# Bidirectional encoder trunk on one core: another order in the last blocks, four joint output operations per head, and a first head that scores a slot later

## The chip, the cores and the metric

The kernel runs on one NeuronCore of a Trainium2 chip. The metric is the device time of one execution in microseconds (us). Engines are named as in the profile: PE is TensorE (PEld its weight loads), DVE is VectorE, ACT is ScalarE, POOL is GpSimd, SP is the engine whose queue issues most DMAs.

## The reference

The input x is 512 tokens by 1024 channels. Two layers are added to it, each as `x = x + layer(x)`, and a last RMSNorm ends it. Layer 0 projects the normed input, runs a gated position mixer and a windowed attention, and projects back. Layer 1, which the change touches, is cut here to what matters:

```python
def hgrn2_direction(q, f_logit, i, lb):        # per head: S, D = 512, 128; chunks
    f = lb + (1.0 - lb) * sigmoid(f_logit); k = 1.0 - f; bcum = cumsum(log(f), within a chunk)
    q_t = q * exp(bcum); k_t = k * exp(-bcum); k_end = k * exp(blast - bcum)
    a = tril(q_t @ k_t.T); o_intra = a @ i
    # state: S = S * exp(blast) + k_end.T @ i;  o_inter = q_t @ S
    return o_intra + o_inter

def odd_layer(x, ...):
    h = rms_norm(x, norm_g); q, f_f, f_b, i, z = split(h @ w_in)      # 16 heads of 128
    o = hgrn2_direction(silu(q), f_f, i) + flip(hgrn2_direction(flip(silu(q)), flip(f_b), flip(i)))
    o = o * rsqrt(mean(o * o, per head) + EPS) * head_norm_g
    return (o * silu(z)) @ w_out

out = rms_norm(x + odd_layer(x, ...), final_norm_g)
```

## The kernel before

Every float32 matrix product is done as three products of parts (hi and lo), on line 207, the "main products". Weights come in pieces of 512 KB: SP issues the load, ACT casts the hi part (L58) and DVE subtracts to get the lo part (L59), some pieces ahead of their use. `t_block` makes 24 main products of 512 columns for one projection of one head, `out_blocks` adds a projection back into x (L254).

Side work is written as generators. Every eighth main product is a slot: `tick` then lets each of up to three side jobs do its next stage, and `yield n` in a job means "n slots from now". So the written order of PE's work is fixed by these numbers; a scheduler then sets the order of each engine's list. Each engine works its list off in order.

In layer 1 (`hgrn`, one job per head) a head needs three `t_block`s, nine slots. Its stages are: a preparation (gate logarithms L608, L611, a scan L614 on DVE, L617, L618, exponentials L622 to L623 on ACT, scalings of keys L628 and L631 on DVE and of queries L630 and L632 on POOL), `yield 7`, scores (L642 to L645) and transposes of keys (L658) with their copies kn (L660), one slot later products L670, one slot later the states u (L678 and L681 on DVE) and products L685, one slot later L689 and L691, then the square (L696), the reduction (L698), the power -0.5 on POOL (L137, L142), the scaling (L700) and the gating (L701), and after four slots the transposes (L705) and the split into hi and lo (L707, L708). For heads 14 and 15 what POOL does is put on DVE (`eng`). Four heads share one pair of value and gate tiles (a group); in each group the main products of the first head come behind those of values and gates.

The end: after head 15 the last two heads are projected by `out_blocks` with `finish` (its squares L151, its sums L155) and `store` (L757, L758), tile of 128 tokens by tile, with DVE's order as written.

Of the kernel before, what the change touches and what calls it, by code (L numbers as in the profile page):

```python
# [10 lines left out]
F32 = mybir.dt.float32  # L11
# [3 lines left out]
AF = mybir.ActivationFunctionType  # L15
ALU = mybir.AluOpType
AX = mybir.AxisListType

P = 128
S = 512  # L20
NT = 4
D = 1024
KT = 8
EPS = 1e-6
# [3 lines left out]
FAR = 1e30  # L28
# [3 lines left out]
class Weights:  # L32
    """Streams weight pieces [128, a, b] with a * b = 1024: DMA, then an exact
    split of every value into two float32r parts (hi + lo)."""
# [50 lines left out]
def tile_encoder(ctx, tc, x, nge, wie, lng, lnb, ws, bs, sink, woe, ngo, wio, gaf, gab, hng, woo, fng, out):  # L85
    nc = tc.nc
    x = x[0]
    out = out[0]
# [8 lines left out]
    def mm_bank():  # L97
        return pm.tile([P, 512], F32, tag="mm", name="mm")
# [4 lines left out]
    W = Weights(tc, wp, dma_ahead=7, split_ahead=3, raw_bufs=4, bufs=4)  # L103

    # ------------------------------------------------ weight order
# [19 lines left out]
    # ------------------------------------------------ constants  # L125
# [14 lines left out]
    def inv_sqrt(v, n, name):  # L140
        r = small.tile([P, n], F32, tag=name + "r", name=name + "r")
        nc.gpsimd.tensor_tensor(out=r, in0=v, in1=mhalf[:, :n], op=ALU.pow)  # L142
        return r
# [5 lines left out]
    def square_half(t, nh, ss, scratch):  # L149
        # (x / 32)^2 summed over 1024 columns: the mean square  # L150
        nc.scalar.activation(scratch, xs[t][:, halves[nh]], AF.Square, scale=1.0 / 32, accum_out=ss[:, nh:nh + 1])  # L151

    def rstd_halves(ss, name):
        v = small.tile([P, 1], F32, tag=name + "v", name=name + "v")
        nc.vector.tensor_scalar(out=v, in0=ss[:, 0:1], scalar1=ss[:, 1:2], scalar2=EPS, op0=ALU.add, op1=ALU.add)  # L155
        return inv_sqrt(v, 1, name)
# [19 lines left out]
    # ------------------------------------------------ blocks of projections  # L176
    # Side work (attention, mixer, recurrence) comes in stages; a stage yields the number of slots of
    # main products to let pass before the next one, so that the tensor engine doesn't wait for it.
# [25 lines left out]
    def mm3(ps, ops):  # L204
        n = len(ops)
        for i, (l, r) in enumerate(ops):
            nc.tensor.matmul(ps, lhsT=l, rhs=r, start=(i == 0), stop=(i == n - 1))  # L207
            count[0] += 1
            if count[0] % SLOT == 0:
                tick()  # L210
# [50 lines left out]
    def split_act(src):  # L261
        """float32 [128, 512] in SBUF -> hi + lo"""
        ahi, alo = act_pair()
        nc.scalar.copy(ahi, src)
        nc.vector.tensor_tensor(out=alo, in0=src, in1=ahi.bitcast(F32), op=ALU.subtract)
        return ahi, alo

    # ================================================ layer 0
# [30 lines left out]
    with ExitStack() as c0:  # L299
# [37 lines left out]
        # the order in which the loads arrive  # L337
# [23 lines left out]
        # distance |s - t| of key column c (s = c - 128) to query row t, out of the window: FAR  # L361
# [13 lines left out]
        # ---- position mixer weights, transposed to [s, g, t]  # L375
# [8 lines left out]
        # ---- v_a and its LayerNorm  # L384
# [22 lines left out]
        # ---- keys and values  # L407
# [18 lines left out]
        # ---- attention  # L426
# [80 lines left out]
        # ---- spatial gating  # L507
# [28 lines left out]
    # ================================================ layer 1  # L536
    l1 = ctx.enter_context(tc.tile_pool(name="l1", bufs=1, reuse_waits="tile"))

    # ---- lower bounds: rows (direction, layer, head) then the head norm's gains, transposed to [d, row]
# [25 lines left out]
    # ---- masks  # L565
# [3 lines left out]
    # scores of a chunk, s on partitions: rows of its first half A hold A -> A, A -> B forwards and the  # L569
    # extra A -> A backwards; rows of its second half B hold B -> A, B -> B backwards and the extra B -> B forwards  # L570
# [12 lines left out]
    # ---- end of layer 0: its last products, with the norm of each tile of tokens as it is complete  # L583
# [5 lines left out]
    sst = {}  # L589
# [12 lines left out]
    def hgrn(h, sq, sg, iv, zv):  # L602
# [30 lines left out]
        yield 7  # L633
# [18 lines left out]
        # ---- states, centred in the middle of each chunk; step j: chunk j forwards, chunk 3 - j backwards  # L652
# [47 lines left out]
        nc.vector.tensor_tensor(out=o2, in0=pov, in1=r.unsqueeze(2).broadcast_to([P, NT, P]), op=ALU.mult)  # L700
        eng.tensor_tensor(out=o2, in0=o2, in1=zv[:, :, hs], op=ALU.mult)  # L701
# [40 lines left out]
    def finish(t, nh):  # L742
        if nh == 0:
            sst[t] = small.tile([P, 2], F32, tag="ss", name="ss")
        junk = l1.tile([P, 512], F32, tag="o2", name="junk", bufs=1)
        square_half(t, nh, sst[t], junk)
        if nh == 1:
            if t:
                store(t - 1)
            scales.append(rstd_halves(sst[t], "nr"))  # L750

    scales = []

    def store(t):
        for cs in halves:
            xv = xs[t][:, cs]
            nc.vector.scalar_tensor_tensor(out=xv, in0=xv, scalar=scales[t], in1=gain2[:, cs], op0=ALU.mult, op1=ALU.mult)  # L757
            nc.sync.dma_start(out=out[ts(t, P), cs], in_=xv)  # L758
# [4 lines left out]
    with tc.manual_schedule(engines={mybir.EngineType.DVE}):  # L763
        out_blocks([acat1[14], acat1[15]], finish)
        store(NT - 1)
# [29 lines left out]
```

## Time and profile before

| | |
|---|---|
| device time, median of 3 runs (lowest to highest) | 1036.95 us (1036.91 to 1037.04) |
| span of the profiled execution | 1035.3 us |
| mean granted clock of PE over the span | 0.997 |
| DMA, fastest of the 40 slices of the span | 322 GB/s |
| stores of the output | 8 of 256 KB, 2.1 us from issue to landing |

The profiled execution's own device time is not among the three runs; what lies around its span is taken from the median, 1.65 us. The page shows the busy share of each engine, and its longer part groups of instructions by line. The views used below are the list of waits (who waited for whom), and the timeline, in which every row is an instruction with its start, its duration, its engine and line, what it writes and reads, and in brackets how long its engine had been idle before it and what ended that.

### The profile page before, as it was taken

The page shows a single profiled execution, that of the slowest core. Times are in us where ns is not written, and L with a number is a line of the kernel's source. Part 1 is how long each engine was busy: PE and PEld are TensorE (multiplying, and loading weights), DVE is VectorE, ACT ScalarE, POOL GpSimd, SP SyncE. Part 2 cuts the span into 40 slices and gives each one's busy share as a digit, 9 for nine tenths or more (in the row PEclk, how much of TensorE's full clock was granted, in tenths as well). Part 3 has the DMA queues.
Part 4 walks back from the last instruction along what each step waited for, and adds up shares of the span by engine and source line. Part 5 has one row for each costly group of instructions (what it writes and reads, how often), then busy time and mean ns, then how long its engine had stood idle before and what let it go on. Part 6 is the DMA issues. An engine that isn't in the chain of part 4 may idle for free.

```text
span 1035.3 us, 13564 instructions
## 1 busy us (share of the span) xinstructions
PE 1012.9 (98%) x5381; PEld 851.9 (82%) x5381; DVE 597.7 (58%) x946; ACT 517.1 (50%) x705; POOL 147.4 (14%) x155
## 2 busy tenths in 40 slices
PE   6999999999999999999999999999999999999996
PEld 5888888888888887888888888888888888878884
DVE  6574677566434464446754546754436764547685
ACT  5333666354222144458743258753257753377742
POOL 1140000000000200004231003322002322012101
PEclk9999999999999999999999999999999999999998
DMA  9243222222233222341212432212432223422102
GB/s 322 85 120 85 81 62 62 82 82 82 82 85 99 85 81 82 100 131 54 85 39 82 122 102 62 63 61 82 122 102 61 62 62 102 122 82 77 47 1 81
DMA packets 109343, 90.05 MB, mean 87 GB/s; under 512 B 2992, under 2 KB 88544, under 8 KB 109280
## 3 DMA queue, kind: packets, MB, share of 16 engines
q1 hardware_dynamic: 109184, 89.14, 28.3%
q8 instruction: 42, 0.69, 0.3%
q14 instruction: 21, 0.17, 0.1%
q0 software_dynamic: 96, 0.04, 0.0%
HBM read 87.08 MB, written 2.10 MB: 86 GB/s over the span
## 4 chain that ended last, share of the span: by engine, by line
PE 89%; ACT 3%; DVE 3%; issue 2%; POOL 1%; DMA 1%; SPq 0%; POOLq 0%; DVEq 0%; ACTq 0%
PE mm L207 74%; PE sm L670 2%; PE sm L642 2%; PE sm L448 1%; PE sm L685 1%; PE sm L487 1%; PE sm L691 1%; PE sm L689 1%; DVE c L614 1%; PE sm L476 1%; PE sm L658 1%; PE sm L705 1%; PE sm L512 1%; PE sm L644 1%; ACT whi L58 1%
## 5 line engine op out<-in xcount | busy, mean ns | idle before, releaser
L59 DVE TENSOR_TENSOR wlo<-wraw,whi 128x1024 fp32r<-128x1024 f32 x156 | 196.9, 1268 | 143.9 <-ACT whi L58 141.5
L58 ACT CAST whi<-wraw 128x1024 fp32r<-128x1024 f32 x156 | 163.1, 1051 | 231.2 <-PE mm L207 215.0
L207 PE MATMUL mm<-hlo,whi 128*128 128x512 f32 x656 | 258.2, 394 | 0.0
L207 PE MATMUL mm<-hhi,wlo 128*128 128x512 f32 x656 | 257.8, 393 | 0.0
L207 PE MATMUL mm<-hhi,whi 128*128 128x512 f32 x656 | 256.5, 391 | 0.0
L207 PEld LDWEIGHTS mm<-hhi,whi 128*128 128x128 f32 x656 | 123.3, 188 | 24.6
L207 PEld LDWEIGHTS mm<-hlo,whi 128*128 128x128 f32 x656 | 123.3, 188 | 24.1
L207 PEld LDWEIGHTS mm<-hhi,wlo 128*128 128x128 f32 x656 | 123.3, 188 | 23.9
L207 PE MATMUL mm<-whi,hhi 128*128 128x512 f32 (+1 forms) x352 | 135.9, 386 | 0.1
L207 PE MATMUL mm<-whi,hlo 128*128 128x512 f32 (+1 forms) x352 | 135.5, 385 | 0.0
L207 PE MATMUL mm<-wlo,hhi 128*128 128x512 f32 (+1 forms) x352 | 135.3, 385 | 0.0
L207 PE MATMUL mm<-whi,ahi 128*128 128x512 f32 x256 | 100.4, 392 | 0.1
L207 PE MATMUL mm<-wlo,ahi 128*128 128x512 f32 x256 | 100.3, 392 | 0.0
L207 PE MATMUL mm<-whi,alo 128*128 128x512 f32 x256 | 100.1, 392 | 0.0
L207 PEld LDWEIGHTS mm<-wlo,hhi 128*128 128x128 f32 x352 | 66.6, 189 | 13.1 <-DVE wlo L59 1.1
L207 PEld LDWEIGHTS mm<-whi,hhi 128*128 128x128 f32 x352 | 66.8, 190 | 12.6 <-ACT hhi L170 0.7
L207 PEld LDWEIGHTS mm<-whi,hlo 128*128 128x128 f32 x352 | 66.5, 189 | 12.0 <-DVE hlo L171 0.3
L254 DVE TENSOR_TENSOR x<-mm,x 128x512 f32<-128x512 f32 x72 | 49.0, 688 | 43.5 <-PE mm L207 43.4
L630 POOL TENSOR_TENSOR sq<-sq,en 128x512 f32<-128x512 f32 x14 | 23.8, 1700 | 266.4 <-ACT en L622 266.4
L207 PEld LDWEIGHTS mm<-whi,ahi 128*128 128x128 f32 x256 | 48.1, 188 | 10.2 <-ACT ahi L707 0.5
L207 PEld LDWEIGHTS mm<-whi,alo 128*128 128x128 f32 x256 | 48.1, 188 | 9.6
L207 PEld LDWEIGHTS mm<-wlo,ahi 128*128 128x128 f32 x256 | 48.1, 188 | 9.5
(176 smaller groups left out, 1377.2 us busy)
## 6 DMA issues: line engine op xcount, KB each, us to landing
wraw<-in_w_in_odd_dram SPq DMA_DIRECT2D x80, 512.0 KB, 3.9
wraw<-in_w_in_even_dram SPq DMA_DIRECT2D x44, 512.0 KB, 4.0
wraw<-in_w_out_even_dram SPq DMA_DIRECT2D x16, 512.0 KB, 3.5
wraw<-in_w_out_odd_dram SPq DMA_DIRECT2D x16, 512.0 KB, 3.5
x<-in_x_dram SPq DMA_DIRECT2D x4, 512.0 KB, 8.3
out_dram<-x SPq DMA_DIRECT2D x8, 256.0 KB, 2.1
pThi<-in_norm_g_even_dram SPq DMA_DIRECT2D x1, 512.0 KB, 5.4
lngb<-in_gmlp_ln_g_dram SPq DMA_DIRECT2D x1, 512.0 KB, 6.1
```

The costliest lines, as they stand in the source:

```text
L58: self.nc.scalar.copy(hi, raw)
L59: self.nc.vector.tensor_tensor(out=lo, in0=raw, in1=hi.bitcast(F32), op=ALU.subtract)
L207: nc.tensor.matmul(ps, lhsT=l, rhs=r, start=(i == 0), stop=(i == n - 1))
L254: nc.vector.tensor_tensor(out=xv, in0=ps, in1=xv, op=ALU.add)
L448: nc.tensor.matmul(pv, lhsT=a[:, ql], rhs=b[:, kv, kr], start=(i == 0), stop=(i == 2))
L476: nc.tensor.transpose(ps[:, ts(n - n0, P)], pr[:, n, ts(j - KEYS[n][0], P)], ident)
L487: nc.tensor.matmul(po[:, n0 * P:n1 * P], lhsT=a[:, j, ts(kv, P)], rhs=b[:, j, :w], start=(j == 0 and i == 0), stop=(j == NT - 1 and i == 2 ...
L512: nc.tensor.matmul(ps[:, ts(n, P)], lhsT=va[n][:, ts(c, P)], rhs=wsT[:, g], start=True, stop=True)
L614: nc.vector.tensor_tensor_scan(out=cf, data0=reset.rearrange("p n t -> p (n t)"), data1=cf, initial=0.0, op0=ALU.mult, op1=ALU.add)
L630: eng.tensor_tensor(out=v8(qb), in0=v8(qf), in1=en[:, 1, :, 0:64], op=ALU.mult)
L642: nc.tensor.matmul(ps[:H, o:o + P], lhsT=kf[:, lo_:mid], rhs=qf[:, lo_:hi_], start=True, stop=True)
L670: nc.tensor.matmul(ps[:, ts(2 * j + d, P)], lhsT=kn[:, jj, d], rhs=iv[:, n, hs], start=True, stop=True)
```

## The change

Three edits. A first head of a group (`hl == 0`) lets eight slots pass before its scores, not seven. A head's output is scaled and gated in four joint DVE operations of 128 columns, one per tile of tokens, in place of L700 and L701. And `finish` and `store` are replaced by `last_blocks`, in which the scaling of a finished tile is shared among DVE, ACT and POOL, the last block of PE is cut in two of 256 columns, and the last store goes out in two halves, one on ACT's DMA queue; ACT's order is now as written there, too. Comments that went are left out here.

```diff
-        yield 7
+        yield 8 if hl == 0 else 7
...
-        nc.vector.tensor_tensor(out=o2, in0=pov, in1=r.unsqueeze(2).broadcast_to([P, NT, P]), op=ALU.mult)
-        eng.tensor_tensor(out=o2, in0=o2, in1=zv[:, :, hs], op=ALU.mult)
+        for n in range(NT):
+            nc.vector.scalar_tensor_tensor(out=o2[:, n], in0=pov[:, n], scalar=r[:, n:n + 1], in1=zv[:, n, hs],
+                                           op0=ALU.mult, op1=ALU.mult)
...
+        def part(t, i, c0, n):
...
+            mm3(ps[:, :n], ops)
+            xv = xs[t][:, c0:c0 + n]
+            nc.vector.tensor_tensor(out=xv, in0=ps[:, :n], in1=xv, op=ALU.add)
+            nc.scalar.activation(junk[:, :n], xv, AF.Square, scale=1.0 / 32, accum_out=sums[t][:, i:i + 1])
+
+        def scale_of(t):
+            v = small.tile([P, 1], F32, tag="nrv", name="nrv")
+            ss = sums[t]
+            nc.vector.tensor_scalar(out=v, in0=ss[:, 0:1], scalar1=ss[:, 1:2], scalar2=EPS, op0=ALU.add, op1=ALU.add)
+            if t == NT - 1:
+                nc.vector.tensor_scalar(out=v, in0=ss[:, 2:3], scalar1=v, scalar2=None, op0=ALU.add)
+            scales[t] = inv_sqrt(v, 1, "nr")
+
+        def store(t):
+            x0, x1 = xs[t][:, :512], xs[t][:, 512:]
+            nc.vector.scalar_tensor_tensor(out=x0, in0=x0, scalar=scales[t], in1=gain2[:, :512], op0=ALU.mult, op1=ALU.mult)
+            nc.sync.dma_start(out=out[ts(t, P), :512], in_=x0)
+            nc.scalar.activation(x1, x1, AF.Copy, scale=scales[t])
+            nc.gpsimd.tensor_tensor(out=x1, in0=x1, in1=gain2[:, 512:], op=ALU.mult)
+            nc.sync.dma_start(out=out[ts(t, P), 512:], in_=x1)
+
+        for t in range(NT):
+            sums[t] = small.tile([P, 4], F32, tag="ss", name="ss")
+            part(t, 0, 0, 512)
+            if t:
+                scale_of(t - 1)
+            if t < NT - 1:
+                part(t, 1, 512, 512)
+            else:
+                part(t, 1, 512, 256)
             if t:
                 store(t - 1)
...
+        t = NT - 1
+        part(t, 2, 768, 256)
+        xg = [l1.tile([P, 512], F32, tag=tag, name="xg", bufs=1) for tag in ("u", "kn1")]
+        nc.vector.tensor_tensor(out=xg[0], in0=xs[t][:, :512], in1=gain2[:, :512], op=ALU.mult)
+        scale_of(t)
+        nc.vector.tensor_tensor(out=xg[1], in0=xs[t][:, 512:], in1=gain2[:, 512:], op=ALU.mult)
+        nc.scalar.activation(xg[0], xg[0], AF.Copy, scale=scales[t])
+        nc.vector.tensor_scalar(out=xg[1], in0=xg[1], scalar1=scales[t], scalar2=None, op0=ALU.mult)
+        nc.sync.dma_start(out=out[ts(t, P), 512:], in_=xg[1])
+        nc.scalar.dma_start(out=out[ts(t, P), :512], in_=xg[0])
```

In the changed kernel the lines from L701 on have other numbers: the joint operation is L701, the transposes of the output L706, the split L708 and L709, the gate's sigmoid L739, and of the end the add L761, the square L762, the sums L767 and L769, the scalings L774 (DVE), L776 (ACT) and L777 (POOL), and of the last tile L794, L796, L797 and L798.

The list of DVE before, from the first head's weight split to the second head's scan (u: states of the first head; sg and c: gates of the second; wlo: a weight piece):

```order
L59 TENSOR_TENSOR wlo<-wraw,whi 128x1024
L681 TENSOR_SCALAR u<-sm,tt 128x128 x2
L678 TENSOR_TENSOR u<-sm,u 128x256
L681 TENSOR_SCALAR u<-u,tt 128x128 x2
L678 TENSOR_TENSOR u<-sm,u 128x256
L681 TENSOR_SCALAR u<-u,tt 128x128 x2
L611 TENSOR_SCALAR sg<-sg,noml,oml 128x512
L614 SCALAR_TENSOR_TENSOR c<-reset,c 128x1040
L617 COPY tt<-c 128x16
L618 TENSOR_TENSOR c<-c,tt 128x8x65
```

The same place in DVE's list of the changed kernel:

```order
L59 TENSOR_TENSOR wlo<-wraw,whi 128x1024
L681 TENSOR_SCALAR u<-sm,tt 128x128 x2
L678 TENSOR_TENSOR u<-sm,u 128x256
L611 TENSOR_SCALAR sg<-sg,noml,oml 128x512
L614 SCALAR_TENSOR_TENSOR c<-reset,c 128x1040
L681 TENSOR_SCALAR u<-u,tt 128x128
L617 COPY tt<-c 128x16
L681 TENSOR_SCALAR u<-u,tt 128x128
L618 TENSOR_TENSOR c<-c,tt 128x8x65
L678 TENSOR_TENSOR u<-sm,u 128x256
L681 TENSOR_SCALAR u<-u,tt 128x128 x2
```

The second head's gate operations and its scan stood behind the last state and now stand between the first and the second. The four groups have the same list there.

ACT's list of the changed kernel at the same place, from the second head's first logarithm L608 (kn: transposed keys of the first head; whi: a weight piece; o: square of the first head's output):

```order
L608 ACTIVATE c<-sg,lb,oml 128x8x64
L739 ACT_TABLE_LOAD
L739 ACTIVATE sg<-mm 128x512
L660 COPY kn_3765<-sm 128x512
L660 COPY kn_3765<-sm 128x256
L58 CAST whi<-wraw 128x1024
L608 ACT_TABLE_LOAD
L608 ACTIVATE c<-sg,lb,oml 128x8x64
L622 ACT_TABLE_LOAD
L622 ACTIVATE en<-c 128x1040
L625 ACTIVATE tt<-tt 128x16
L623 ACTIVATE c<-c 128x1040
```

Before, the two copies kn and the cast stood ahead of the sigmoid and its table load, and the square L696 stood ahead of L622; now L696 comes behind L623, the sigmoid of the third head's query and one more cast.

POOL's list of the changed kernel at the end (nrr: power of a tile's mean square; x: a tile of the output):

```order
L142 TENSOR_TENSOR nrr<-nrv,mhalf 128x1
L777 TENSOR_TENSOR x_70<-x_70,gain_7759 128x512
L142 TENSOR_TENSOR nrr<-nrv,mhalf 128x1
L777 TENSOR_TENSOR x_71<-x_71,gain_7759 128x512
L142 TENSOR_TENSOR nrr<-nrv,mhalf 128x1
L777 TENSOR_TENSOR x_72<-x_72,gain_7759 128x512
L142 TENSOR_TENSOR nrr<-nrv,mhalf 128x1
```

Before, POOL had the four powers L142 there and nothing between them.

## Rows read from the trace of the kernel before

**Rows 1.** The page, part 1: busy us (share of the span) x instructions.

```profile
PE 1012.9 (98%) x5381; PEld 851.9 (82%) x5381; DVE 597.7 (58%) x946; ACT 517.1 (50%) x705; POOL 147.4 (14%) x155
```

**Rows 2.** List of waits, PE: line, released by; us in total, times, longest us.

```profile
PE sm L642 <- POOL sq L632: 4.1, 4, 1.0
```

**Rows 3.** Timeline of PE, first group: start, us, engine, line, out<-in, [idle before <-releaser].

```profile
470.62 0.32 PE L642 MATMUL sm<-sq,sg 128*64 128x128 f32 x1 [1.03 <-POOL sq L632]
...
474.68 1.50 PE L670 MATMUL sm<-iv,kn 128*128 128x128 f32 x12
...
480.60 0.38 PE L689 MATMUL sm<-u,sq 128*128 128x128 f32 x2
...
481.86 0.48 PE L207 MATMUL mm<-hlo,whi 128*128 128x512 f32 x1
...
491.02 0.60 PE L705 MATMUL sm<-ident,o 128*128 128x128 f32 x4
```

**Rows 4.** Timeline of ACT, first group.

```profile
472.48 0.82 ACT L608 ACTIVATE c<-sg,lb,oml 128x512 f32<-128x512 f32 x1
473.20 0.84 ACT L660 COPY kn<-sm 128x512 f32<-128x512 f32 x2
474.64 1.04 ACT L58 CAST whi<-wraw 128x1024 fp32r<-128x1024 f32 x1 [0.60 <-PE mm L207]
475.70 1.28 ACT L738 ACT_TABLE_LOAD   x1
477.00 0.60 ACT L738 ACTIVATE sg<-mm 128x512 f32<-128x512 f32 x1
...
485.98 1.08 ACT L623 ACTIVATE c<-c 128x1040 f32<-128x1040 f32 x1
```

**Rows 5.** Timeline of DVE, first group.

```profile
475.72 1.23 DVE L59 TENSOR_TENSOR wlo<-wraw,whi 128x1024 fp32r<-128x1024 f32 x1 [1.78 <-ACT whi L58]
476.86 0.73 DVE L681 TENSOR_SCALAR u<-sm,tt 128x128 f32<-128x128 f32 x2
477.62 0.42 DVE L678 TENSOR_TENSOR u<-sm,u 128x256 f32<-128x256 f32 x1
...
479.25 0.60 DVE L681 TENSOR_SCALAR u<-u,tt 128x128 f32<-128x128 f32 x2
...
480.22 2.32 DVE L614 TENSOR_TENSOR_SCAN c<-reset,c 128x1040 f32<-128x1040 bf16 x1
...
482.78 0.70 DVE L618 TENSOR_TENSOR c<-c,tt 128x520 f32<-128x520 f32 x1
483.40 0.68 DVE L698 TENSOR_REDUCE hss<-o 128x4 f32<-128x512 f32 x1
```

**Rows 6.** Timeline: POOL in the first group, and beside DVE behind it.

```profile
484.43 1.03 POOL L142 TENSOR_TENSOR hrr<-hrv,mhalf 128x4 f32<-128x4 f32 x1 [9.11 <-DVE hrv L137]
...
489.29 1.30 POOL L701 TENSOR_TENSOR o<-o,zv 128x512 f32<-128x512 f32 x1
...
554.80 1.21 DVE L59 TENSOR_TENSOR wlo<-wraw,whi 128x1024 fp32r<-128x1024 f32 x1
555.03 2.13 POOL L701 TENSOR_TENSOR o<-o,zv 128x512 f32<-128x512 f32 x1 [0.87 <-DVE o L700]
```

**Rows 7.** Timeline of the end, all engines.

```profile
1014.60 0.69 DVE L700 TENSOR_TENSOR o<-sm,hrr 128x512 f32<-128x512 f32 x1 [1.19 <-POOL hrr L142]
...
1016.64 0.63 PE L705 MATMUL sm<-ident,o 128*128 128x128 f32 x4 [0.91 <-DVE o L701]
...
1020.29 0.63 ACT L151 ACTIVATE junk<-x 128x512 f32<-128x512 f32 x1 [2.30 <-DVE x L254]
...
1022.09 0.56 POOL L142 TENSOR_TENSOR nrr<-nrv,mhalf 128x1 f32<-128x1 f32 x1 [7.52 <-DVE nrv L155]
...
1026.11 0.39 PE L207 MATMUL mm<-whi,alo 128*128 128x512 f32 x1
...
1030.60 1.42 DVE L757 SCALAR_TENSOR_TENSOR x<-x,nrr,gain 128x512 f32<-128x512 f32 x2 [0.66 <-POOL nrr L142]
```

More of the change, by code (lines that the diff above doesn't have):

```diff
@@ L741, in tile_encoder, with last_blocks @@
     nc.sync.dma_start(out=gain2, in_=fng.partition_broadcast(P))
-    def finish(t, nh):
-        if nh == 0:
-            sst[t] = small.tile([P, 2], F32, tag="ss", name="ss")
+    def last_blocks(heads):
+        pieces = [W.take() for _ in range(2)]
         junk = l1.tile([P, 512], F32, tag="o2", name="junk", bufs=1)
-        square_half(t, nh, sst[t], junk)
-        if nh == 1:
+        sums, scales = {}, {}
+        def part(t, i, c0, n):
+            ps = mm_bank()
+            ops = []
+            nh, cs = c0 // 512, slice(c0 % 512, c0 % 512 + n)
+            for k, (ahi, alo) in enumerate(heads):
+                whi, wlo = pieces[nh]
+                a, b = ahi[:, ts(t, P)], alo[:, ts(t, P)]
+                ops += [(a, whi[:, k, cs]), (a, wlo[:, k, cs]), (b, whi[:, k, cs])]
+            mm3(ps[:, :n], ops)
[25 more added lines that the diff above has]
+                part(t, 1, 512, 256)
@@ L748, in finish @@
             if t:
                 store(t - 1)
[L750 to L758, printed above, removed]
+        t = NT - 1
+        part(t, 2, 768, 256)
+        xg = [l1.tile([P, 512], F32, tag=tag, name="xg", bufs=1) for tag in ("u", "kn1")]
@@ L762, in tile_encoder @@
     tick_until(lambda: 15 in acat1)
-    with tc.manual_schedule(engines={mybir.EngineType.DVE}):
-        out_blocks([acat1[14], acat1[15]], finish)
-        store(NT - 1)
+    with tc.manual_schedule(engines={mybir.EngineType.DVE, mybir.EngineType.Activation}):
+        last_blocks([acat1[14], acat1[15]])
 _INS = ['x', 'norm_g_even', 'w_in_even', 'gmlp_ln_g', 'gmlp_ln_b', 'gmlp_w_s', 'gmlp_b_s', 'attn_sink',
```

## The prediction

> **What bounds the kernel now.** I read the engine shares of the page first: the TensorE (PE) is busy for 1012.9 of 1035.3 us, every other engine for 58% or less [rows 1]. So a microsecond counts only where PE waits, or after PE's last product. The list of waits, for PE, has one entry in layer 1 that repeats: the score products L642 wait for POOL's second scaling of the queries (L632), 4.1 us in four waits, 1.0 each at most [rows 2]. They are the first heads of the four groups; the other twelve heads score without a wait. The PE timeline around the first of them shows a gap of 1.03 us before L642 at 470.62 [rows 3]. Last I read the end: PE waits once more, 0.91 us, for the last head's output (L705 at 1016.64), starts its last product at 1026.11, and VectorE (DVE) ends its last scaling at 1030.60 + 1.42 = 1032.02 [rows 7]; the rest to 1035.3 is the last store and the program's end. So the change aims at three places where time really is lost: 4.1 us at the first heads, about 1 us at the last head, and 6 us behind the last product.
>
> **First heads, one slot later.** Eight main products go ahead of the scores. Forty of them take 491.02 - 481.86 = 9.16 us [rows 3], so eight take 1.83 us, more than the 1.03 us of the gap: the wait for POOL goes. The price stands in the instruction order. The first head's later steps (states, L670; u, L681 and L678; L689 and L691) also come one slot later, but the second head's preparation does not. Before, DVE did the whole u chain of the first head (476.86 to 479.25 + 0.60 = 479.85) and then the second head's L611 and scan L614 [rows 5]. Now L611, L614, L617 and L618 stand inside the u chain. DVE and ACT work through their lists in order, so I replay them from the trace, on the clock of the first group.
>
> PE: without a new wait L689 would start at 480.60 - 1.03 + 1.83 = 481.40 [rows 3], L691 and the other products around it take 481.86 - 480.60 = 1.26, and the main products would go on at 482.66.
>
> ACT: nothing is changed up to L608, which ends at 472.48 + 0.82 = 473.30. Then before came the copies kn (L660) [rows 4]; now a table load (1.28) and the gate's sigmoid (0.60, as L738 had) come first, so kn is complete at 473.30 + 1.28 + 0.60 + 0.84 = 476.02. The next weight cast L58 (1.04) ends at 477.06. PE wants kn's first part for L670 at 474.68 - 1.03 + 1.83 = 475.48 and gets it some 0.3 later, a small wait that the next one swallows.
>
> DVE: the weight split L59 stands ahead of u and waits for that cast, as it did before (475.72, released by ACT); u starts 476.86 - 475.72 = 1.14 later, at 478.20. L678 follows after 477.62 - 476.86 = 0.76, at 478.96; L611, behind it, needs the second sigmoid's L608, which ends at 477.06 + 1.28 + 0.82 = 479.16, so that it starts at about 479.4, and takes some 0.45 to the scan. From the scan's start to L618 it is 482.78 - 480.22 = 2.56 [rows 5], with two u scalings of 0.30 between; then L618 about 0.62, L678 about 0.46 and the last pair L681 0.60: 479.85 + 2.56 + 0.60 + 0.62 + 0.46 + 0.60 = 484.69. L691 can follow at about 484.8 and the main products at 485.0, where 482.66 was wanted: a wait of 2.3 us in place of the 1.03. Against before, where eight products more would have brought PE to 481.86 + 1.83 = 483.69, each group is 1.3 us later. If DVE overlaps its small operations better than I add them, u ends 0.3 earlier, and it is 1.0.
>
> A second chain holds PE to the same. ACT's exponentials wait for L618 (now at about 483.7): table load 1.28, L622 and L623 some 1.1 each [rows 4], load 1.28, sigmoid 0.60, cast 1.04, and only then the square L696 (0.60): 490.7. DVE's L59 before the reduction ends at about 491.3, the reduction takes about 0.7 [rows 5], L137 0.2, POOL's power 1.0 [rows 6], and the joint operations come at 493.3 to 494.7. PE is at the transposes at 485.0 + 9.16 = 494.2, its fourth at 494.5: a wait of 0 to 0.4. So a quicker u alone would not win the time back. I take 1.25 a group, from 1.0 to 1.7; the order is the same in all four, so 4 x 1.25 = +5.0 us (+4.0 to +6.8).
>
> **Output of a head in four joint operations.** L700 (0.69) and the gating (1.30 on POOL, 0.68 on DVE for heads 14 and 15) become four operations of 128 columns on DVE. None of that form stands in the trace; from the 512-wide L700 (0.69) a quarter each gives at least 0.17, a 128-wide scaling that reads PSUM (two L681 in 0.73) at most 0.41 [rows 5 and 7]. I take 0.35, as this is the nearest form: 1.4 us for four. For heads 0 to 13 it costs nothing: DVE is busy 58%, PE does not wait for these outputs before, and POOL loses 1.3 us of work. For head 15 it counts: before, 1014.60 to 1016.64; now the fourth output is there at about 1016.0 and the fourth transpose starts at 1016.2, where it started at about 1016.97: 0.75 us earlier (0.5 to 1.3).
>
> **The last blocks.** They are in another order, too: eight instead of twelve products of head 14 stand ahead of the first product with head 15. The four missing ones (0.23 each, 0.9 us) come behind it, so that PE's last product ends at about 1026.5, as before (1026.11 + 0.39), and the 0.75 us are gone. Behind it DVE has less to do: half of each store's scaling is ACT's and POOL's. But POOL's list now alternates L142 and L777, so each tile's power waits for the multiplication of the tile before. PE ends tile 1's second block 24 products of 0.23 before its end, at 1021.0; its add (0.7, as L700) and its square with the sum read out (0.8) bring 1022.5. From there: ACT's scaling of tile 0 0.60, L777 1.30 (POOL's L701 has that shape, [rows 6]), L142 0.56 [rows 7], to 1025.0; tile 1 likewise (its power is used after tile 2's squares, 1025.2), 1025.2 + 0.6 + 1.3 + 0.56 = 1027.7; then DVE scales tile 2 (0.7), and only behind that adds the last quarter, which PE had ready since 1026.5: 1028.8. Then L794 reads two SBUF operands beside L777 of tile 2 (1028.4 to 1029.7). In the trace such a pair was not run together: POOL's L701 took 2.13 instead of 1.30 when it met L59 [rows 6], about the rest of L59 longer. So L794 ends at 1030.4; L767 and L769 0.3, L142 0.6 with its start, the last scalings 0.6: 1032.0, where before had 1032.02. I take 0 for the end. Best case, with no collision and short operations, -1.5; worst, with each L777 at 2.13 (two on the chain, 1.7, less the 0.9 of slack at L794) and the two last stores sharing the DMA engines (0.8, a store's 256 KB at the 322 GB/s of the page's fastest slice), some +1.5.
>
> The Trainium skill, page "SBUF — State Buffer", section "Who interferes with whom", says that a VectorE instruction with two SBUF inputs and a GpSimd instruction that reads SBUF exclude each other for the whole instruction. The pair in [rows 6] agrees: 555.03 + 2.13 is 1.15 us after L59's end at 556.01. By the rule L794 waits as reckoned, and without it the end would be 0.9 us earlier.
>
> **Sum.** The profiled execution has a span of 1035.3; the runs' median is 1036.95, so 1.65 us lie around it. 1035.3 + 5.0 + 0 + 1.65 = 1041.95 us.
>
> **Rivals.** (1) The wait just goes: 4 x 1.03 = -4.1 us, 1032.8, faster. For it: the gap of the list of waits is real, and u, ready at 479.85 for a last use at about 481.7, had 1.8 us of room. Against: scan, L617 and L618 add 3.2 us. It decides if u, with all that is put into it, ends before 482.4, 2.3 us earlier than I reckon: 0.07. (2) u comes late by just what was won, 1.25 us a group less than I reckon: 1036.95, no change; it needs L59 ahead of u not to wait for the late cast, which the row at 475.72 speaks against: 0.07. (3) More comes with it: after the late transposes the second head's scores follow at once, where a slot lay between, and its last transposes wait until DVE has emptied the PSUM bank of the first ones; at 1.9 us a group and +1 at the end it gives 1036.95 + 8.6 = 1045.5: 0.08. (4) The end runs at PE's pace, because POOL's products are shorter than reckoned: -1.5, with the groups' +5.0: 1040.5; it lies within my forecast.
>
> **How the numbers follow.** The forecast (with 4) has 0.78. Its own range is 1035.3 + 1.65 + 4.0 - 1.5 = 1039.4 to 1036.95 + 6.8 + 1.5 = 1045.3 if all ends meet; I cut it to 1039.0 to 1044.2, which leaves out rivals 1 and 2 and most of 3, about 0.2. About 0.2% (2.1 us) is what a measurement of this kernel can tell from no change. Faster by that: 0.08. Within: 0.08, mostly rival 2. Slower: 0.84.
>
> **What would show it.** In the profile after: PE's wait at L642 for POOL gone from the list, and four new waits of about 2 us at L689 or L691, released by DVE's u (L681), with scan L614 between the u rows; L660 behind a sigmoid; a wait of some tenths at L706. At the end: L777 of about 1.3 us on POOL ahead of each L142, and the last scaling ending about 1032 plus the shift. No PE wait at L691, and a span of about 1031, would make my replay of DVE's list wrong; a span of 1033 with the waits there would mean an end that is 7 us shorter than I think.

## The result

The changed kernel took 1042.45 us (median of four runs, 1041.74 to 1042.72) against 1036.93 of the kernel before in the same session: a ratio of 1.0052, 95% interval 1.0038 to 1.0067. It is slower, by 5.5 us, where 5.0 were forecast. Its profiled execution took 1042.44 us with a span of 1040.4; all starts below are of profiled executions, counted from the start of the span. The traces of the experiments e1 and e9 are not used, since every main product in them took several times its usual duration; their timed runs are.

The engine shares [rows 1] have hardly moved; PE has most of its time, as before:

```profile
PE 1017.1 (98%) x5387; PEld 853.6 (82%) x5387; DVE 598.1 (57%) x992; ACT 519.5 (50%) x711; POOL 132.0 (13%) x144
```

The list of waits does show the change (line, what it waited for, us in all, times, longest). The entry for POOL's scaling L632 of [rows 2] is gone; u has come in its place:

```profile
PE sm L689 <- DVE u L681: 3.3, 4, 0.8
PE sm L706 <- DVE o L701: 1.0, 1, 1.0
PE sm L670 <- ACT kn L660: 0.8, 4, 0.2
```

The timeline of PE in the first group answers to [rows 3] (start, us, line, out<-in, and in brackets the idle time and what ended it):

```profile
475.69 1.60 PE L670 MATMUL sm<-iv,kn 128*128 128x128 f32 x12 [0.19 <-ACT kn L660]
...
481.74 0.38 PE L689 MATMUL sm<-u,sq 128*128 128x128 f32 x2
...
483.86 0.49 PE L689 MATMUL sm<-u,sq 128*128 128x128 f32 x2 [0.84 <-DVE u L681]
484.18 0.42 PE L691 MATMUL sm<-u,sq 128*128 128x128 f32 x2
...
493.33 0.39 PE L207 MATMUL mm<-hhi,whi 128*128 128x512 f32 x1
493.56 0.67 PE L706 MATMUL sm<-ident,o 128*128 128x128 f32 x4
...
496.34 0.47 PE L207 MATMUL mm<-hlo,whi 128*128 128x512 f32 x1
```

The list gives 0.84 us to the wait for u, but the starts tell more: from the first of the products with u to the last it is 484.18 - 481.74 = 2.44 us, where the trace of before has 1.11 (from the 480.60 of [rows 3] to 481.71). So 1.33 us are lost here, some more at L670, and the 1.03 of [rows 2] is won. At the transposes (L706, 493.56) the list names no wait; the second head's scores now follow them at once, and from the last main product ahead of both to the first behind them it is 496.34 - 493.33 = 3.01 us. ACT and DVE in the same stretch, against [rows 4] and [rows 5]:

```profile
474.57 0.60 ACT L739 ACTIVATE sg<-mm 128x512 f32<-128x512 f32 x1
475.06 0.86 ACT L660 COPY kn<-sm 128x512 f32<-128x512 f32 x2
...
478.03 0.72 DVE L681 TENSOR_SCALAR u<-sm,tt 128x128 f32<-128x128 f32 x2
...
479.58 2.32 DVE L614 TENSOR_TENSOR_SCAN c<-reset,c 128x1040 f32<-128x1040 bf16 x1
...
483.46 0.60 DVE L681 TENSOR_SCALAR u<-u,tt 128x128 f32<-128x128 f32 x2
...
492.71 1.13 DVE L701 SCALAR_TENSOR_TENSOR o<-sm,hrr,zv 128x128 f32<-128x128 f32 x4 [1.14 <-POOL hrr L142]
```

The sigmoid stands ahead of kn, and the second head's scan (479.58, 2.32 us) stands inside the first head's u chain, which ends at 483.46 + 0.60 = 484.06 instead of 479.85. The square of the output (L696) of the second to fourth head comes 0.78 us later than before in the first group, 1.90 in the second, 2.95 in the third, 4.02 to 4.08 in the last: the groups cost 4.08 us, and not all of that is the slot's (e3).

The end, against [rows 7]. The square of the last head starts at 1015.98 (before: 1011.90), so from there to the span's end it is 24.4 us after and 23.4 before, 1.0 more:

```profile
1029.94 1.27 POOL L777 TENSOR_TENSOR x<-x,gain 128x512 f32<-128x512 f32 x1 [0.91 <-ACT x L776]
...
1030.21 0.28 PE L207 MATMUL mm<-whi,alo 128*128 128x256 f32 x1
...
1031.18 0.55 POOL L142 TENSOR_TENSOR nrr<-nrv,mhalf 128x1 f32<-128x1 f32 x1
...
1031.76 0.75 DVE L774 SCALAR_TENSOR_TENSOR x<-x,nrr,gain 128x512 f32<-128x512 f32 x1 [0.89 <-POOL nrr L142]
...
1032.56 1.26 POOL L777 TENSOR_TENSOR x<-x,gain 128x512 f32<-128x512 f32 x1 [0.83 <-ACT x L776]
...
1032.76 1.61 DVE L794 TENSOR_TENSOR xg<-x,gain 128x512 f32<-128x512 f32 x1
...
1034.90 0.93 POOL L142 TENSOR_TENSOR nrr<-nrv,mhalf 128x1 f32<-128x1 f32 x1 [1.07 <-DVE nrv L769]
...
1035.86 0.49 DVE L798 TENSOR_SCALAR xg<-xg,nrr 128x512 f32<-128x512 f32 x1 [0.44 <-POOL nrr L142]
...
1036.61 0.37 ACTq L800 DMA_DIRECT2D out_dram<-xg  x1
```

PE's last product has moved by 1030.21 - 1026.11 = 4.10, just with the groups. Behind it the last tile's first product with the gains (L794) takes 1.61 us beside POOL's L777, the last power (L142) 0.93 beside L796, where those of the tiles before took 0.55 to 0.57.

### The profile page after: what moved, and what is told of

The parts are those of the page before. It is cut to its first block, busy times and chain, and to the rows that moved or that the text cites. A ratio compares the mean times of both kernels' runs of the same rounds, so it can differ in the third digit from the quotient of the medians.

```text
span 1040.4 us, 13601 instructions
## 1 busy us (share of the span) xinstructions
PE 1017.1 (98%) x5387; PEld 853.6 (82%) x5387; DVE 598.1 (57%) x992; ACT 519.5 (50%) x711; POOL 132.0 (13%) x144
## 4 chain that ended last, share of the span: by engine, by line
PE 84%; ACT 7%; DVE 5%; issue 2%; POOL 1%; DMA 1%; POOLq 0%; SPq 0%; ACTq 0%; DVEq 0%
PE mm L207 71%; DVE c L614 2%; PE sm L670 2%; ACT L739 1%; PE sm L448 1%; PE sm L487 1%; ACT whi L58 1%; PE sm L642 1%; PE sm L685 1%; DVE wlo L59 1%; PE sm L689 1%; PE sm L691 1%; PE sm L476 1%; PE sm L706 1%; ACT sg L739 1%
## 5 line engine op out<-in xcount | busy, mean ns | idle before, releaser
L59 DVE TENSOR_TENSOR wlo<-wraw,whi 128x1024 fp32r<-128x1024 f32 x156 | 192.0, 1235 | 143.0 <-ACT whi L58 140.6
L207 PEld LDWEIGHTS mm<-hhi,wlo 128*128 128x128 f32 x656 | 123.3, 188 | 24.4
L207 PE MATMUL mm<-whi,ahi 128*128 128x512 f32 (+1 forms) x258 | 100.8, 391 | 0.0
L207 PE MATMUL mm<-wlo,ahi 128*128 128x512 f32 (+1 forms) x258 | 100.8, 391 | 0.0
L207 PE MATMUL mm<-whi,alo 128*128 128x512 f32 (+1 forms) x258 | 100.3, 390 | 0.0
L254 DVE TENSOR_TENSOR x<-mm,x 128x512 f32<-128x512 f32 x64 | 43.9, 688 | 42.7 <-PE mm L207 42.6
```

Source lines behind the costliest of these rows:

```text
L59: self.nc.vector.tensor_tensor(out=lo, in0=raw, in1=hi.bitcast(F32), op=ALU.subtract)
L254: nc.vector.tensor_tensor(out=xv, in0=ps, in1=xv, op=ALU.add)
```

## The experiments

Each was timed in five rounds beside the kernel before (1036.67 us in the session of e1 to e4, 1036.89 in that of e5 to e8, 1036.88 in that of e9 to e11).

| run | us | ratio to before, 95% interval |
|---|---|---|
| e1 changed, without the slot | 1038.98 | 1.0020, 1.0011 to 1.0029 |
| e2 slot alone | 1050.99 | 1.0138, 1.0125 to 1.0152 |
| e3 joint operations alone | 1036.54 | 0.9999, 0.9990 to 1.0007 |
| e4 changed, second head a slot later too | 1039.97 | 1.0030, 1.0018 to 1.0043 |
| e5 e4, scan held behind u | 1041.61 | 1.0049, 1.0036 to 1.0062 |
| e6 e3, first heads' queries on DVE | 1033.12 | 0.9967, 0.9955 to 0.9979 |
| e7 e1, no multiplications on POOL at the end | 1037.94 | 1.0011, 1.0002 to 1.0020 |
| e8 e1, last store on SP's queue | 1038.94 | 1.0021, 1.0012 to 1.0030 |
| e9 slot and joint operations | 1039.64 | 1.0028, 1.0017 to 1.0040 |
| e10 new last blocks alone | 1038.47 | 1.0018, 1.0009 to 1.0027 |
| e11 first heads' queries on DVE alone | 1033.67 | 0.9971, 0.9960 to 0.9982 |

**e1, the slot taken back**

```diff
-        yield 8 if hl == 0 else 7
+        yield 7
```

> The changed kernel with the slot taken back: the first heads are scored after 7 slots again, the joint output operations and the new last blocks stay. Theory (the slot costs 4.08 us over the four groups, the last blocks 1.0, the joint operations nothing): the four waits of 1.03 us at the score products for POOL's scaling are back, no wait at u's products, and the time is 1036.93 + 1.0 = 1037.9 us. Rival A (the last blocks cost nothing by themselves and were only pushed by the late groups): 1036.9. Rival B (the slot costs nothing and what lies around it is late through the output operations): 1042.4.

Measured: 1038.98 us. The slot costs 1042.45 - 1038.98 = 3.5 us of the 5.5, and the rest costs 2.3, not the 1.0 that the theory gave it. So neither rival is right. The 1.0 was the end's difference against before, and the joint operations had paid a part of it (e3).

**e2, the slot alone**

```diff
-        yield 7
+        yield 8 if hl == 0 else 7
```

> The kernel before with the slot alone: first heads scored after 8 slots, the output in its old form (a scaling on DVE, the gating on POOL), the old last blocks. Theory: u's wait comes as in the changed kernel (+4.08 in all), and the old output form, which in the changed kernel's trace would end at about 492.71 + 0.69 + 1.30 + 0.1 = 494.8 where PE wants it at 493.3 to 493.6, adds a wait of about 1.3 us at the transposes of each group's first head: 1036.93 + 4.1 + 5.2 = 1046.2 us, with four such waits for POOL in the list. Rival A (no coupling of slot and output form): 1041.0 and no wait at these transposes. Rival B (the slot alone is a gain of its wait): 1032.8.

Measured: 1050.99 us, 14 us slower, more than any theory had. The coupling is there, and larger than reckoned. From the list of waits, and the timeline of POOL and DVE ahead of the first transposes:

```profile
PE sm L705 <- POOL o L701: 7.9, 4, 2.0
```

```profile
493.15 1.22 DVE L59 TENSOR_TENSOR wlo<-wraw,whi 128x1024 fp32r<-128x1024 f32 x1
...
493.38 2.11 POOL L701 TENSOR_TENSOR o<-o,zv 128x512 f32<-128x512 f32 x1 [0.87 <-DVE o L700]
...
494.29 1.49 DVE L611 TENSOR_SCALAR sg<-sg,noml,oml 128x512 f32<-128x512 f32 x1
```

PE waits 2.0 us for each first head's output, not 1.3: the gating on POOL (L701) meets the weight split L59 on DVE and takes 2.11 instead of the 1.30 of [rows 6], and DVE's L611 behind it takes 1.49, where it took 0.54 elsewhere. From the last main product ahead of the first transposes to the first behind the scores, it is 5.05 to 5.10 us in the second to fourth group and 6.63 in the first, where the changed kernel takes 3.0: 9.8 us more in all. The 1.5 that the first group has more are the clock's, in this row of the view of windows (stretch, its length, busy us and instructions of PE, PEld, DVE, ACT and POOL, granted clock, DMA share, GB/s):

```profile
497.00:499.00 2.00, 2.00 (x27) 1.88 (x25) 1.37 (x3) 0.00 (x0) 0.00 (x0) 0.50 0.23 84
```

Behind the wait, in which PE did nothing for 2.0 us, the granted clock fell from 1.00 to 0.50 (the lower of its two levels, 1.2 of 2.4 GHz), and the scores ran at that pace. In the other three groups it stayed at 1.00 behind the same wait; why it fell in the first alone is open. So in the changed kernel the joint operations hide most of the slot's harm.

**e3, the joint operations alone**

```diff
-        nc.vector.tensor_tensor(out=o2, in0=pov, in1=r.unsqueeze(2).broadcast_to([P, NT, P]), op=ALU.mult)
-        eng.tensor_tensor(out=o2, in0=o2, in1=zv[:, :, hs], op=ALU.mult)
+        for n in range(NT):
+            nc.vector.scalar_tensor_tensor(out=o2[:, n], in0=pov[:, n], scalar=r[:, n:n + 1], in1=zv[:, n, hs], ...)
```

> The kernel before with the joint output operations alone. Theory: no PE wait changes for heads 0 to 14; the last head's transposes come 0.75 us earlier, and the end of the kernel before follows PE, so that the time is 1036.93 - 0.7 = 1036.2 us, and the wait at the last transposes falls from 0.91 to some 0.2 us. Rival (more work on DVE delays other steps, four small operations cost more than one large): 1037.5 or more, with new waits for DVE.

Measured: 1036.54 us, no difference that can be told. Its trace has two effects that work against each other. From the first head's square to the last's it takes 0.7 us more (0.2 at each of the three changes of group), and from the last head's square to the end it takes 1034.4 - 1012.08 = 22.3 us instead of 23.4: the last scalings start at 1029.73 instead of 1030.60 [rows 7]. At a change of group a weight load of PE (PEld) waits for a weight split; then PE's last product and these scalings:

```profile
555.96 0.19 PEld L207 LDWEIGHTS mm<-wlo,hhi 128*128 128x128 f32 x1 [0.34 <-DVE wlo L59]
...
1026.16 0.39 PE L207 MATMUL mm<-whi,alo 128*128 128x512 f32 x1
...
1029.73 1.41 DVE L758 SCALAR_TENSOR_TENSOR x<-x,nrr,gain 128x512 f32<-128x512 f32 x2 [0.66 <-POOL nrr L142]
```

The wait of 0.34 us is the joint operations' price: four of them take 1.13 us of DVE (553.65 to 554.78) where L700 alone took 0.69, and the split L59 stands behind them. The kernel before has no such wait there, the changed kernel has it again (557.30). At the end, PE's last product has not moved, so the gain is DVE's: the first add behind the split of the output starts 1018.63 - 1012.08 = 6.55 us behind the last head's square, where before had 1019.50 - 1011.90 = 7.60, and by these two traces the end before hangs on DVE's adds and scalings, not on PE. The traces of e6 and e11 repeat the pair: 1031.9 - 1009.58 = 22.3 us with joint operations, 1032.0 - 1008.60 = 23.4 without. The expectation had the wait at the last transposes falling to 0.2 us; the list has 0.97, since between u's last product and these transposes there are now 10 main products instead of 17. The eight instead of twelve early products of head 14 stand in this trace too; they come with the joint operations, not with the new last blocks.

**e4, the second head prepared a slot later, too**

```diff
+        if hl == 1:
+            yield 1
...
-        yield 8 if hl == 0 else 7
+        yield 8 if hl == 0 else 6 if hl == 1 else 7
```

> The changed kernel with the second head of each group prepared a slot later, too (it waits one slot ahead of its first step and is scored after 6 slots instead of 7, so at the same product as before). On DVE and ACT every step then stands in the order of the kernel before; the first head's u chain is again ahead of the second head's scan. Theory (the cost is the scan inside the u chain, not the slot): no wait at u's products, none at the scores, the groups gain their 4 x 1.03 us, and with 1.0 for the last blocks the time is 1036.93 - 4.1 + 1.0 = 1033.8 us. Rival A (the slot itself is late, whatever stands in the list): 1042. Rival B (the second heads have no slot to give and wait for their scores instead of the first): about 1037.9 to 1039, with four waits at the scores for POOL in the second heads.

Measured: 1039.97 us. The expectation was wrong in its premise: the scheduler had put the scan back into the chain, only one u pair later. The timeline of DVE and PE:

```profile
480.10 2.32 DVE L616 TENSOR_TENSOR_SCAN c<-reset,c 128x1040 f32<-128x1040 bf16 x1
...
481.73 0.38 PE L691 MATMUL sm<-u,sq 128*128 128x128 f32 x2
...
482.33 0.40 DVE L680 TENSOR_TENSOR u<-sm,u 128x256 f32<-128x256 f32 x1
...
482.76 0.60 DVE L683 TENSOR_SCALAR u<-u,tt 128x128 f32<-128x128 f32 x2
...
483.16 0.49 PE L691 MATMUL sm<-u,sq 128*128 128x128 f32 x2 [0.38 <-DVE u L683]
483.49 0.42 PE L693 MATMUL sm<-u,sq 128*128 128x128 f32 x2
```

u ends at 483.36, the six products take 1.76 us instead of 2.44, and each group costs 0.2 to 0.6 us instead of 0.8 to 1.1. That fits the theory in size, but does not test it.

**e5, the scan held behind u**

```diff
# beside the lines of e4
+        if hl == 1:
+            nc.vector.tensor_scalar(out=c[:, 0, 0, 0:1], in0=last_u[0], scalar1=0.0, scalar2=None, op0=ALU.mult)
         nc.vector.tensor_tensor_scan(out=cf, ...)
...
+        if hl == 0:
+            last_u[:] = [u[:, 2, 1, 0:1]]
```

> As the fourth experiment (slot kept, second head's preparation one slot later, new last blocks), and the second head's scan now really behind the first head's u chain on DVE: a one-element multiplication by zero takes u's last value into the scan's reset column, so that the scan can't be put ahead. In the fourth experiment the scan still stood inside the chain (480.10 to 482.42, between u's second and third pair), and PE waited 0.38 us by the list, some 0.65 us by the starts of the six products (1.76 where the kernel before took 1.11). Theory (the scan inside the chain is what makes u late): u ends at about 480.9, no wait at u's products is left, and the groups come to -1.09 + 0.36 (late kn) = -0.7 us each against the kernel with the slot taken back (1038.98): 1036.1 us. Rival A (the chain of the second head's exponentials ahead of the square on ACT then holds the output): the wait turns up at the transposes instead, 0.5 to 0.8 us in each group, and the time stays at 1039 to 1040. Rival B (u was late by the late weight cast alone): 1040 with the wait at u's products unchanged.

Measured: 1041.61 us: the theory's time is wrong; rival A is right in kind, and its loss is larger than the 0.5 to 0.8 us that it gave. The list of waits, and the timeline of DVE, POOL and PE:

```profile
PE sm L713 <- DVE o L708: 4.7, 5, 1.0
```

```profile
480.06 0.60 DVE L686 TENSOR_SCALAR u<-u,tt 128x128 f32<-128x128 f32 x2
...
480.88 2.33 DVE L619 TENSOR_TENSOR_SCAN c<-reset,c 128x1040 f32<-128x1040 bf16 x1
...
481.04 0.38 PE L696 MATMUL sm<-u,sq 128*128 128x128 f32 x2
...
482.15 0.39 PE L698 MATMUL sm<-u,sq 128*128 128x128 f32 x2
...
489.94 1.21 DVE L59 TENSOR_TENSOR wlo<-wraw,whi 128x1024 fp32r<-128x1024 f32 x1
...
490.12 1.91 POOL L142 TENSOR_TENSOR hrr<-hrv,mhalf 128x4 f32<-128x4 f32 x1
...
492.07 1.13 DVE L708 SCALAR_TENSOR_TENSOR o<-sm,hrr,zv 128x128 f32<-128x128 f32 x4 [0.92 <-POOL hrr L142]
...
492.57 1.01 PE L713 MATMUL sm<-ident,o 128*128 128x128 f32 x4 [0.95 <-DVE o L708]
...
495.63 0.47 PE L207 MATMUL mm<-hlo,whi 128*128 128x512 f32 x1
```

u ends at 480.66, before PE asks for it; the six products take 1.11 us again and no wait for u is left. u starts as late as in the changed kernel (477.34 against 478.03, with this whole trace 0.69 earlier from the first head's gates on), so the late cast alone is not the cause. So the scan inside the chain is what made u late: that much is shown. But the time is not won. Now the transposes (L713) wait for the output, 0.95 us by the list; from the last main product ahead of them (491.23) to the first behind the scores (495.63) it is 4.40 us where the changed kernel has 3.01, so 1.39 are lost, all that u had cost. The power on POOL (L142) takes 1.91 us instead of 1.03, since the weight split L59 (489.94 to 491.15) has come to stand beside it; in the changed kernel that split ran elsewhere and the power took 1.03. The edit moved a sigmoid and with it the weight cast on ACT ahead, and so this split: a side effect that was not foreseen. The second chain of the prediction, square, reduction, power, output, is thus real and has no slack here. What the time would be without this meeting, no run shows.

**e6, the first heads' queries on DVE (on top of e3)**

```diff
-        eng = nc.vector if h >= 14 else nc.gpsimd
+        eng = nc.vector if h >= 14 or hl == 0 else nc.gpsimd
```

> The kernel before with the joint output operations (the third experiment, 1036.54 us), no slot, old last blocks, and the first heads' query scalings on DVE instead of POOL. In the trace of before POOL's two scalings run beside DVE's two (467.25 to 470.57); four of 0.69 us on DVE, the first two from 467.25, the other two behind the exponential's end at 468.32, end at about 469.98, 0.6 us earlier. Theory (PE's wait at the first heads' scores is worth its size if it goes without moving anything else): the wait of 1.03 falls to about 0.4 in each group, the time to 1036.54 - 4 x 0.6 = 1034.1 us. Rival A (u or the output is late next, as with the slot): 1036.5, with waits at u's products or at the transposes. Rival B (the whole wait goes): 1032.4.

Measured: 1033.12 us, faster than the kernel before by a ratio of 0.9967 (0.9955 to 0.9979) and the fastest of all. The list of PE's waits, and the first and last of four rows of DVE ahead of the first scores:

```profile
PE sm L642 <- DVE sq L632: 1.2, 4, 0.3
```

```profile
467.23 0.69 DVE L628 TENSOR_TENSOR sg<-sg,en 128x512 f32<-128x512 f32 x1 [1.90 <-ACT en L622]
...
469.04 0.69 DVE L632 TENSOR_TENSOR sq<-sq,c 128x512 f32<-128x512 f32 x1
```

The four scalings follow each other at 0.60 us and end at 469.73; the wait falls to 0.29 us. The gain, 3.4 us against e3, is a little more than 4 x (1.03 - 0.29) = 3.0. The list of PE's waits shows no new one; no step was moved past another head's steps here.

**e7 and e8, the new end without POOL's multiplications, or with the last store on SP's queue (on top of e1)**

```diff
# e7
-            nc.scalar.activation(x1, x1, AF.Copy, scale=scales[t])
-            nc.gpsimd.tensor_tensor(out=x1, in0=x1, in1=gain2[:, 512:], op=ALU.mult)
+            nc.vector.scalar_tensor_tensor(out=x1, in0=x1, scalar=scales[t], in1=gain2[:, 512:], op0=ALU.mult, op1=ALU.mult)
# e8
-        nc.scalar.dma_start(out=out[ts(t, P), :512], in_=xg[0])
+        nc.sync.dma_start(out=out[ts(t, P), :512], in_=xg[0])
```

> The changed kernel without the slot (1038.98 us) and with both halves of the stores of tiles 0 to 2 scaled on DVE; POOL has only the powers there, ACT only the squares; the last tile stays as in the changed kernel. Theory (POOL's multiplications hold the powers and the last tile's first product): a tile's power no longer waits for the multiplication of the tile before (1027.22 to 1028.52, 1029.94 to 1031.21 in the changed kernel), tile 2 is scaled about 1.4 us earlier, and the first products of the last tile take 0.68 instead of 1.61 us, while DVE gets 0.7 more work for tile 2: the end comes about 1.6 us earlier, 1037.4 us. Rival A (the last tile's halves and the store on ACT's queue are the cost): 1039.0. Rival B (DVE then is the bound): 1038.5 or more, with the last scaling behind a busy DVE.

> The changed kernel without the slot (1038.98 us) and with the last store on SP's queue, too, instead of ACT's. In the changed kernel it landed 2.8 us after its issue on ACT's queue, where stores on SP's queue landed after 2.0. Theory (a store costs more on ACT's queue): it lands 0.8 us sooner after its issue, which comes 0.1 to 0.4 later behind the other store, so 0.4 to 0.7 us in all: 1038.4 us. Rival (two stores that end together share the DMA engines wherever they are issued): landing stays near 2.8 us and the time at 1039.0.

Measured: e7 1037.94 us, 1.0 less than e1 where 1.6 were expected; e8 1038.94, no change. The timeline of e7's end:

```profile
1028.96 0.68 DVE L793 TENSOR_TENSOR xg<-x,gain 128x512 f32<-128x512 f32 x1
...
1030.17 0.93 POOL L142 TENSOR_TENSOR nrr<-nrv,mhalf 128x1 f32<-128x1 f32 x1 [2.91 <-DVE nrv L769]
```

L793 (L794 in the changed kernel) takes 0.68 us instead of 1.61 once POOL has no multiplication beside it. The last power still takes 0.93 beside L795. From the last head's square to the end it is 1035.7 - 1011.95 = 23.75 us, still 1.4 more than the old end with joint operations (22.3): 0.8 up to the end of the last scaling, 0.6 behind it. Which part of the last tile's longer chain costs the 0.8 is not tested. The view of DMA issues for the last tile's stores, first of e8, then of the changed kernel (count, KB each, median us from issue to landing):

```profile
out_dram<-xg SPq DMA_DIRECT2D x2, 256.0 KB, 2.3
```

```profile
out_dram<-xg SPq DMA_DIRECT2D x1, 256.0 KB, 2.0
out_dram<-xg ACTq DMA_DIRECT2D x1, 256.0 KB, 2.8
```

The time is the rival's, the landing is not (2.3 us, not 2.8): it is 2 x 2.3 in all on the one queue against 2.0 + 2.8 on two. If the first store took 2.0 us on the one queue as well (an estimate), the second took 2.6; it was issued 0.44 us behind the first instead of 0.24, so it landed no sooner. Both kernels end 3.6 to 3.8 us behind the last issue; e3 ends 1034.4 - 1031.14 = 3.3 us behind its last scaling.

**e9 and e10, the parts put together**

e9 is e3 with the slot's line of e2. e10 is the kernel before with the new last blocks and nothing else.

> The kernel before with the slot and the joint output operations, and the old last blocks: the changed kernel without its last blocks. The order of DVE's u chain and scan is that of the changed kernel. Theory (the parts add up once the output is in joint operations): the groups come to 1015.98 us at the last head's square as in the changed kernel, and behind it stand the 22.3 us of the third experiment (1034.4 - 1012.08) instead of 24.4: a span of 1038.3, a time of 1040.2 us. Rival A (the late groups by themselves push the end, whatever the last blocks): 1042.4. Rival B (the slot costs only what the list of waits names, 4 x (0.84 + 0.2 - 1.03)): 1036.6 to 1037.

> The kernel before with the new last blocks alone (old output form, no slot). From the last head's square to the end the runs so far took 23.4 us (before), 22.3 (with joint operations), 24.4 to 24.65 (with joint operations and new last blocks). Theory (the new last blocks are 2.1 us longer by themselves, because each tile's power stands behind a multiplication on POOL and the last tile is scaled in a longer chain, and the old output form costs its 1.1 on top): 25.5 us, a time of 1036.9 + 2.1 = 1039.0 us. Rival A (the end follows PE's last product, which no version moved, and the output form no longer matters): 24.4, 1037.9 us. Rival B (the new last blocks cost only in company of the joint operations): 1036.9.

Measured: e9 1039.64 us, 0.6 under the theory and far from both rivals: the slot costs 1039.64 - 1036.54 = 3.1 us with joint operations, 3.5 by e1. e10 1038.47 us; its end takes 1037.2 - 1011.86 = 25.3 us (theory 25.5), 1.9 more than before's by the trace and 1.6 by the medians. So the parts add up, but for the slot with the old output form (e2).

**e11, the first heads on DVE without joint operations**

The diff is that of e6, on the kernel before; the first heads' gating then runs on DVE as well.

> The kernel before with the first heads' query scalings, and these heads' gating, on DVE instead of POOL; all else as before (the other heads gate on POOL). Theory (the gain of the sixth experiment is the wait at the first heads' scores, 0.29 instead of 1.03 us, and doesn't need the joint operations): 1036.9 - 4 x 0.74 = 1034.0 us, with waits of 0.3 at the scores for DVE. Rival A (without the joint operations the outputs of other heads then come late at their transposes): 1035 to 1037 with new waits at the transposes for POOL. Rival B (no gain without the joint operations): 1036.9.

Measured: 1033.67 us, as the theory said. The gain is that of the wait at the scores and does not need the joint operations; e6 is 0.6 us faster still, which is within what these intervals can't tell apart.

## Why the prediction came out right, point by point

The time (1041.95 forecast, 1042.45 measured), the sign and the cause in the groups are right. That the number came so close is in part luck: by the traces the slot costs 3.4 us where 5.0 were reckoned, and 1.7 that were put at nothing, 0.7 for the joint operations and 1.0 for the end, make up for it.

- **The wait at L642 goes, and u's takes its place: right.** Order and cause are as replayed, and e5 shows the cause: with the scan behind u no wait for u is left. **Mis-sized:** the sum had 1.25 us a group, 5.0 in all, and 4.0 at the least; measured are 4.08 with the joint operations' 0.7 in it, so 3.4 for the slot (3.5 by e1, 3.1 by e9). u ended at 484.06, not 484.69, as DVE's operations start ahead of the end of the one before: the scan started at 479.58, the estimate had about 479.85. By the starts of the six products the new wait is 1.33 us, not 2.3; the late kn adds 0.36 (475.69 for 475.33 at the pace of the products before), a wait that the next one did not swallow.
- **A quicker u alone would not win the time back: right in e5** (1041.61), by a loss of 1.39 us at the transposes. That there the power stood beside a weight split the prediction did not see. In the changed kernel itself the chain came out as reckoned: the joint operations end at 492.71 + 1.13 = 493.84, as the transposes run (from 493.56), with a wait of 0.1 at most where 0 to 0.4 was said.
- **Joint operations at 0.35 us each: near.** Four took 1.13, not 1.4, and the fourth transpose of the last head came 1.0 us earlier, net of the groups (1020.03 - 4.08 against 1016.97), where 0.75 (0.5 to 1.3) was said. **That they cost nothing for heads 0 to 13 is wrong:** it was argued from DVE's mean load and from waits for the outputs alone, but behind them on DVE stands a weight split that PE wants, and at each change of group it is late (0.34 us at 555.96 in e3), 0.7 in all. With the slot they are worth 1050.99 - 1039.64 = 11 us, since POOL's gating would have stood in the second chain and been held there by L59; the prediction did not say so.
- **The end costs 0: wrong, it costs 1.0.** L794 was held as forecast, by 0.93 us, and ended at 1034.37 - 4.08 = 1030.29 (forecast 1030.4). The step that failed is the one behind it, sums, power and last scalings in 1.6 us to 1032.0: they took 2.21, as L142 was itself held by L796 (0.93 instead of 0.55), and the last scalings ended at 1036.58 - 4.08 = 1032.50, and the two stores, 0.24 us apart, landed 0.5 later; the prediction had that only in its worst case. That a power can be held stood in the trace of before: L142 took 1.99 us at 552.17, beside L59 (552.06 to 553.29), and 1.01 to 1.03 for most heads. Also wrong is where the missing early products come from (the joint operations, e3), and that the last head's earlier output is lost: at the old end it was worth 1.1 us through DVE. Against that end the new last blocks cost 2.1 us (24.4 - 22.3), 1.6 to 2.4 by the times of e10 and of e1 against e3.
- **The rivals.** That the wait just goes (0.07) is refuted by the waits at u, that the net is zero by 4.08 us. More than forecast (1.9 a group) did not come, and the end did not run at PE's pace (1.0 longer, not 1.5 shorter).

The whole account by the traces: joint operations +0.7 in the groups and -1.1 at the end, slot 4.08 - 0.7 = +3.4, last blocks +2.1, together +5.1, the difference of the two spans (1040.4 - 1035.3); the medians give +5.5.

The Trainium skill, page "SBUF — State Buffer", section "Who interferes with whom", has one engine of VectorE and GpSimd wait for the whole instruction of the other where both want the shared port, and says that a VectorE instruction with at most one SBUF input contends only in its two-port modes, which a scaling by scalars can use. The runs agree: L794 1.61 beside POOL's multiplication and 0.68 without it, the power 1.91 beside L59 and 0.93 beside L796, but 0.55 to 0.56 beside the adds that read PSUM; L611, a scaling by scalars, 1.49 behind POOL's gating.

## What to carry to other kernels

When a head is scored later, move with it all that was ordered against it, or take the wait away where it arises: the first heads' two query scalings, moved to DVE (e6, e11), won about what the slot lost. Read a wait's cost from the starts of the instructions around it, since the list named 0.84 us where 1.33 were lost. Before a step is given to POOL, see what DVE does at that moment with two SBUF operands, and run every part of a change alone and in pairs: here one part hid 11 us of another's harm.

## What was not expected of the hardware

A power of one number per partition on POOL (128x1), among the smallest work of the kernel, is held like a large one: 0.55 us became 0.93 beside a multiplication on DVE, and one of 128x4 went from 1.03 to 1.91. It works both ways within one stretch of e2: L59 held L701 (2.11 for 1.30), and L701 then held L611 (1.49 for 0.54), a scaling with one SBUF tensor and two scalars. And 256 KB stores landed 2.0 us after their issue one at a time, but 2.3 on the mean where two were issued 0.4 us apart on one queue, and 2.8 for the second of two 0.2 us apart on two.
